# A hybrid encoder layer on one core: an expert's index made apart from its gather, the router written in order by hand, and another issue order for the mixer

## The chip, the cores and the metric

The kernel runs on one core of one Trainium2 chip. The metric is the time of one execution of the whole program on the device, in microseconds. Engines are named as in the profile: PE (matrix multiply; PEld its weight loads), DVE (vector), ACT (activation functions), POOL (the general engine, which also makes the descriptors of gathers and scatters), SP (which issues the plain DMAs).

## The reference

One layer on a sequence of 1024 tokens of width 1024, all in float32 (norms, biases and gains left out here):

```
n = rms_norm(h);  proj = n @ w_in                    # 1024 x 6720
c = silu(centred_dwconv(proj[:, :4608], 7 taps))     # q, k, v, x, B, C
o = gated_delta(q, k, v) both directions             # 8 heads of 128, chunks of 64
y = ssd(x, B, C) both directions                     # 16 heads of 64 in 2 groups
h = h + [norm(o) * silu(gate), norm(y * silu(z))] @ w_out

n2 = rms_norm(h);  aff = softmax(n2 @ w_router)      # 1024 x 16
vals, idx = top_k(aff.T, 128)                        # each expert takes 128 tokens
for e in range(16):
    xs = n2[idx[e]]
    ye = (silu(xs @ w_gate[e]) * (xs @ w_up[e])) @ w_down[e] * vals[e]
    h[idx[e]] += ye
return rms_norm(h)
```

## The kernel before

Products in float32 are made as three passes of a 32-bit matmul form over a high and a low half: ACT makes the high half of a tile (`whi`, or `place` in the experts), DVE subtracts it from the raw tile to get the low half (`wlo`), and PE multiplies high by high, high by low and low by high.

**The mixer.** The program is a list of small jobs, each with a slot, entered with `at(slot, fn, ...)`; a job that yields goes on later. `flush("mixer")` does not follow the slots: it issues the jobs in the order of a table of 3602 numbers, `ORDER["mixer"]`, and `tc.manual_schedule()` around it keeps that order on every engine. The transposed input `n_hi`, `n_lo` is made first (lines 325 to 361): x tiles and the small parameter rows are loaded by SP, PE transposes them, ACT and DVE split them. Then 53 blocks of 128 columns of `w_in` go through `w_load` (SP), `w_split` (ACT `whi`, DVE `wlo`; each block in two halves, 106 in all) and `w_unit` (line 242 on PE, eight times six matmuls for a block). Between them run the convolutions (`cacc`, `cpr`), the delta rule and the scan. The scan's decay tiles `E` are loaded from `rowsD` by SP, masked by POOL in two instructions, put through Exp by ACT and used by DVE; of the 32 tiles, 16 belong to each of two groups. Last come the output projection in six rounds (line 1289), the residual and the router's logits `lg`.

**The router.** After the table's last job the probabilities `aff` are made, and 15 rounds `j` search for each expert's threshold: DVE makes a mask of three trial values (`msk`), PE sums it over tokens (line 1533, eight small matmuls), DVE picks (`best`) and makes the next trial. This part of the code stands outside `manual_schedule`, so there the framework's scheduler orders the instructions. Beside the rounds the first expert's first six weight tiles are split: ACT makes `hi` (`EARLY`), and DVE makes `lo` in 12 halves of 128x512 (`rest`, the function's calls come from the rounds). Then the positions `posx` are worked out.

**The experts.** `flush("moe")` orders its jobs by slot, 17 slots an expert. `rt(e)` makes a one-hot tile `oh` (eight DVE instructions), counts on PE (line 1580), makes the index `idx` and the value on DVE (`ax`), and issues the gather of the expert's 128 rows on POOL (`place<-n2D,idx`). `xt` transposes the rows, `gm` multiplies by gate and up, `ht` transposes, `dm` multiplies by down, `ys` scatters. Weight tiles of 512 KB come through one pool of 46 tiles: `give` returns a tile and issues the next load on SP.

Of the kernel before, what the change touches and what calls it, by code (L numbers as in the profile page):

```python
# [20 lines left out]
L = 1024  # L21
# [22 lines left out]
        "c-l>v1FU9EvxU35tGlY-v2EM7ZQHhO+qP}nwr$(it@HlLmzyVR)#}x?_nyflXELLdQQ=i2<&;)Y6)CH{3a40wQn3_>;;9%yY!zCCQDIdC6-UKY"  # L44
        "5mjUrP^hA-#G*vviB)_RMN%S_OGQ%&RdSU>6ko_Gq*4ilgerH?Q>Z*Duga%Vs?;h;kQORUkn}=Y*-Ed9sB)6hs&ql}tE56vQ8J;Js-rT<%%BR0"
        "G71GnnN@L>No7$BRJI`5h4MmHRY+A(g;fc;%_LiyRY_G!l~!f`qvHSbGOCiQEM7%b6|W|$rD_NJ>Z*pMnyRzpW~!d5FSD$wE0k58R2T98(IDsz"
        "|2vme6I55#O?6j2R8JKO8cEYwHBr4(Q%TK*R;s1ytNN&Zs<mpPdaG%wtu#|qe>FgSq8g|MsljT93JvX4d(}Zrl8qTcXy~Yhso`pbx-O?O5Dvma"
        "1PB9RVW^5I9tk4DR5enKQlr%vHCaW0v1*)}suDpohz@gAbeO4*L0Pz>W~*6hj*1HDAsu9Z7!Xs)2$>)j#D+K!7iO!uDjsBp_>ce+LKe88ZmFy="
        "UR@P(LJ}wk*HjKsE|{n0tIaAKY*q_ZQb-DkVUe1ywy4CA401zq$OF?=dH5|&3P=fgAs^(20+0$)!(z2W{Zu#AFCjZr5Gui6RSEtn1xwX3wOs8~"
        "D^x*PsVYK6NCRo1FsxFQVYOPL0M@E?YO7kWHmHq4P57g#KoxNf$7LReLQn(@REACJkV3cwyOjk8JJfEqN9|Jw)G64j_N$_BP@RS|a28HLF*pf_"  # L50
        ")nRo+*rtxELHZ<|gF0|r9aAUNNp(t{hYN5KPOIWj0!qReRZ6r=U54$dD%60>@EXpk^YUvstFFOyxB=DSg1V%t!7I1|SK$q86|W9&;T^n(4{%Xk"
        "R#((bxCQs%wh97w)E#wK-BWkqBYc8;sut9Sx=;`93wKq0xUcT32I38&5j=tisuPqJzYAZXF*Jck>XCY=9;>F%3?9Q{Nl&0TJW(y+DYS%E@K8Nb"
# [56 lines left out]
def trunk(ctx, tc, x, norm1_w, w_in, conv_w, conv_b, gdn_A_log, gdn_dt_bias, gdn_norm_w,  # L109
# [1376 lines left out]
    act(lg, lg, AF.Exp)  # L1486
    act(warm, mhalf[:, :1], AF.Silu)
    den = hp.tile([128, NT], F32, name="den")
    V.tensor_reduce(den, lg, axis=AX.X, op=OP.add)
# [17 lines left out]
    def rest(parts, cols, last):  # L1507
        raw, hi, lo = parts
        tt(V, lo[:, cols], raw[:, cols], hi.bitcast(F32)[:, cols], OP.subtract)
        if last:  # L1510
            give(raw)
# [322 lines left out]
```

## Time and profile before

| | us |
|---|---|
| median of 3 runs (1672.53, 1676.93, 1685.21) | 1676.93 |
| the profiled execution | 1671.89 |
| its span, first to last instruction | 1670.2 |
| PE busy in the span (93%) | 1550.8 |
| DVE, ACT, POOL busy | 1211.5, 982.0, 730.0 |

A row of the timeline has the start, the time (of all instructions of a merged row, which overlap a little), the engine, line and operation, out<-in with the program's names, and in brackets the idle time of the engine before it and what ended that. PEclk is the granted clock of PE as a share of 2.4 GHz; 0.50 is the lower of its two levels, 1.2 GHz.

### The profile page before, as it was taken

What the parts mean: (1) busy time and instruction counts of PE and PEld (TensorE: products, weight loads), DVE (VectorE), ACT (ScalarE), POOL (GpSimd) and SP (SyncE); (2) the same over time, 40 slices, a digit from 0 to 9 for tenths busy, and PEclk for the clock granted to TensorE, in tenths of its full rate; (3) what the DMA queues carried; (4) which work ended last, traced back from release to release, by engine and by line L of the source; (5) the groups of instructions that cost most, each with busy time, mean ns of one, the idle gap of its engine ahead of it and who ended that gap; (6) DMA issues with size and microseconds to landing.
All of it is one profiled execution on the core that took longest, in us unless ns stands there. A gap on an engine that the chain in (4) does not pass through costs nothing. (4 is left out here: it accounts for less than half of the span.)

```text
span 1670.2 us, 23559 instructions
## 1 busy us (share of the span) xinstructions
PE 1550.8 (93%) x8290; PEld 1264.7 (76%) x8290; DVE 1211.5 (73%) x2045; ACT 982.0 (59%) x1788; POOL 730.0 (44%) x533
## 2 busy tenths in 40 slices
PE   5989999999999999998989999998996499899997
PEld 4768888888889888887765687687885377677774
DVE  4686768686767677757779976864556598789875
ACT  5476485858586767465542574243455177677764
POOL 1285263647454654425898877713032011111112
PEclk9999999999999999999999999999997599999999
DMA  4322223223231322222332245457787289999955
GB/s 137 98 60 43 45 65 68 75 56 87 42 98 28 105 70 63 39 70 95 108 101 70 67 135 172 150 183 263 256 284 291 111 311 372 329 382 375 389 184 213
DMA packets 174784, 254.20 MB, mean 152 GB/s; under 512 B 54370, under 2 KB 112027, under 8 KB 174667
## 3 DMA queue, kind: packets, MB, share of 16 engines
q1 hardware_dynamic: 170202, 236.45, 42.3%
q0 software_dynamic: 4464, 16.25, 3.8%
q8 instruction: 65, 1.06, 0.3%
q14 instruction: 53, 0.43, 0.1%
HBM read 221.01 MB, written 31.65 MB: 151 GB/s over the span
## 5 line engine op out<-in xcount | busy, mean ns | idle before, releaser
L242 PE MATMUL pj<-n,whi 128*128 128x512 f32 x1664 | 482.5, 412 | 9.8 <-ACT whi L129 7.5
L242 PEld LDWEIGHTS pj<-n,whi 128*128 128x128 f32 x1664 | 301.0, 190 | 79.2 <-ACT whi L129 11.1
L242 PE MATMUL pj<-n,wlo 128*128 128x512 f32 x832 | 263.4, 398 | 3.6 <-DVE wlo L123 3.5
L123 DVE TENSOR_TENSOR place<-place 128x1024 fp32r<-128x1024 f32 (+1 forms) x182 | 208.0, 1184 | 27.8 <-ACT place L129 27.8
L126 DVE SCALAR_TENSOR_TENSOR cacc<-pj,cols,cacc 128x1023 f32<-128x1023 f32 (+2 forms) x156 | 199.3, 1278 | 22.8 <-POOL cacc L123 20.1
L123 POOL TENSOR_TENSOR cacc<-cacc,cpr 128x1021 f32<-128x1021 f32 x60 | 145.7, 2429 | 153.4 <-ACT cacc L129 81.0
L1648 PE MATMUL pj<-place 128*128 128x512 f32 x768 | 198.3, 410 | 2.0 <-DVE place L123 1.3
L129 ACT ACTIVATE place<-place 128x1024 fp32r<-128x1024 f32 (+1 forms) x181 | 181.5, 1053 | 16.8 <-issue 8.5
L242 PEld LDWEIGHTS pj<-n,wlo 128*128 128x128 f32 x832 | 156.2, 189 | 45.8 <-DVE wlo L123 8.3
L1648 PEld LDWEIGHTS pj<-place 128*128 128x128 f32 x768 | 144.5, 192 | 40.6 <-DVE place L123 5.3
L123 DVE TENSOR_TENSOR n<-n 128x1024 fp32r<-128x1024 f32 x64 | 84.3, 1327 | 68.9 <-ACT n L129 40.7
L1591 POOL DMA_INDIRECT place<-n2D,idx x16 | 17.4, 1088 | 259.4 <-ACT place L129 93.7
L129 ACT ACTIVATE n<-n 128x1024 fp32r<-128x1024 f32 x64 | 66.7, 1056 | 104.1 <-DMA n<-in_w_out_dram 55.2
L123 DVE TENSOR_TENSOR wlo<-wraw,whi 128x512 fp32r<-128x512 f32 x106 | 96.7, 914 | 15.0 <-ACT whi L129 14.9
L1289 PE MATMUL pj<-n 128*128 128x512 f32 x384 | 97.4, 408 | 4.1 <-DVE n L123 4.1
L129 ACT ACTIVATE whi<-wraw 128x512 fp32r<-128x512 f32 x106 | 65.8, 625 | 57.7 <-PE pj L242 47.5
L129 ACT ACTIVATE place<-g 128x512 fp32r<-128x512 f32 (+1 forms) x48 | 26.9, 561 | 110.4 <-PE g L1612 106.2
L1289 PEld LDWEIGHTS pj<-n 128*128 128x128 f32 x384 | 72.5, 191 | 24.2 <-DVE n L123 5.8
L129 ACT ACTIVATE cpr<-pj,cols 128x1021 f32<-128x1021 f32 x60 | 66.5, 1109 | 26.6 <-PE pj L242 16.9
L129 ACT ACTIVATE u<-c,bt 128x128 f32<-128x128 f32 x128 | 39.6, 363 | 60.1 <-DVE ud L123 58.4
L123 POOL TENSOR_TENSOR ex<-N,nm 128x512 f32<-128x512 f32 x48 | 62.2, 1304 | 14.6 <-PE g L785 9.9
L123 DVE TENSOR_TENSOR E<-E,tb_dt 128x1024 f32<-128x1024 f32 x32 | 56.9, 1790 | 15.5 <-ACT E L129 15.3
(328 smaller groups left out, 3202.9 us busy)
## 6 DMA issues: line engine op xcount, KB each, us to landing
place<-in_w_gate_dram SPq DMA_DIRECT2D x64, 512.0 KB, 9.3
place<-in_w_up_dram SPq DMA_DIRECT2D x64, 512.0 KB, 8.7
place<-in_w_down_dram SPq DMA_DIRECT2D x64, 512.0 KB, 9.8
wraw<-in_w_in_dram SPq DMA_DIRECT2D x106, 256.0 KB, 3.3
E<-rowsD SPq DMA_DIRECT2D x32, 512.0 KB, 3.8
n<-mixD SPq DMA_DIRECT2D x64, 256.0 KB, 3.4
n<-in_w_out_dram SPq DMA_DIRECT2D x64, 256.0 KB, 4.4
dec<-rowsD SPq DMA_DIRECT2D x16, 512.0 KB, 7.7
```

The costliest lines, as they stand in the source:

```text
L123: eng.tensor_tensor(o, a, b, op=op)
L126: V.scalar_tensor_tensor(o, a, s, b, op0=op0, op1=op1, **kw)
L129: S.activation(o, i, f, **kw)
L242: T.matmul(pj[c0][:, hs], lhsT=w[:, d % 4, :], rhs=nn[d][:, hs], start=(d == 0 and a == 0), stop=(d == ND - 1 and a == 2))
L1289: T.matmul(wst["po", r][t], lhsT=m[:, 0, ts], rhs=w[:, 1, :], start=(k == k0 and a == 0), stop=(k == k1 - 1 and a == 2))
L1591: nc.gpsimd.indirect_dma_start(out=ex["xs", e], out_offset=None, in_=n2D[:, :], in_offset=ex["idx", e])
L1648: T.matmul(po, lhsT=xT[:, j, d % 4, :], rhs=wt[k][:, HALF[dd]], start=(d == 0 and a == 0), stop=(d == ND - 1 and a == 2))
```

## The change

Three things change together.

- The table `ORDER["mixer"]` has the same 3602 entries in another order; most jobs stand a little elsewhere.
- The router's code stands inside `tc.manual_schedule()`. The rounds `j` 2 to 13 take one half of `rest` each, the rounds 0 and 1 the two steps of `aux` (the parts of `aff` in a shorter format).
- The gather is a job of its own, `gx(e)`. `rt` of the experts 0 to 3 runs right behind the positions, one after the other with short pauses; `gx` of 0 and 1 stands between them, `gx` of the later experts where the gather stood before.

```
-        "c-l>v1FU9EvxU35tGlY-v2EM7ZQHhO+qP}nwr$(it@HlLmzyVR)#}x?_nyflXELLdQQ=i2<&;)Y6)CH{3a40wQn3_>;;9%yY!zCCQDIdC6-UKY"
+        "c-lRe1CX@65`}|KI+@S5ZQHhO+qP}nwr$(CZCm&3)L*xrI*rqvytBJCyR$-QVTBjrgc3$L5lX}Y@kD45UW65KL?jVGL=`bWY!OjJ7A&L)BLad%"
...
+    with tc.manual_schedule():
         act(lg, lg, AF.Exp)
         act(warm, mhalf[:, :1], AF.Silu)
...
         for j in range(15):
             tt(V, msk3, aff[:, :, None, :].to_broadcast(S4), trialf[:, None].to_broadcast(S4), OP.is_ge)
-        if j > 1 and halves:
-            rest(*halves.popleft())
+            if j < 2:
+                src = res if j else aff
+                V.tensor_copy(aux[:, :, :, 2 + j], src)
+                tt(V, aux[:, :, :, 4] if j else res, src, aux[:, :, :, 2 + j], OP.subtract)
+            elif halves:
+                rest(*halves.popleft())
...
-    res = hp.tile(SE, F32, name="res")
-    V.tensor_copy(aux[:, :, :, 2], aff)
-    tt(V, res, aff, aux[:, :, :, 2], OP.subtract)
-    V.tensor_copy(aux[:, :, :, 3], res)
-    tt(V, aux[:, :, :, 4], res, aux[:, :, :, 3], OP.subtract)
...
     def rt(e):
...
-        yield 6.0
+        yield 0.5 if e < 4 else 6.0
...
-        yield 0.2
+        ex["idx", e], ex["val", e] = bass.IndirectOffsetOnAxis(ap=idx[:, :1], axis=0), ax[:, 6:7]
+
+    def gx(e):
         ex["xs", e] = take()
-        ex["idx", e], ex["val", e] = bass.IndirectOffsetOnAxis(ap=idx[:, :1], axis=0), ax[:, 6:7]
         nc.gpsimd.indirect_dma_start(out=ex["xs", e], out_offset=None, in_=n2D[:, :], in_offset=ex["idx", e])
...
-    at(-30, rt, 0)
-    at(-29, rt, 1)
+    for e in range(4):
+        at(-30 + 1.9 * e, rt, e)
+        if e < 2:
+            at(-28.8 + 1.9 * e, gx, e)
...
             if e + 2 < NE:
-                at(b + 2, rt, e + 2)
+                if e > 1:
+                    at(b + 2, rt, e + 2)
+                at(b + 8.7, gx, e + 2)
```

ACT's queue at the start, behind the splits of the last input tiles (`n`; `whi` are halves of projection weights, `Rf` 128x48 holds the decay parameters that SP loads, `O` is a copy of the first projected block). Before:

```order
L129 ACTIVATE n<-g,cols 128x512 x2
L129 ACTIVATE whi<-wraw 128x512
L129 ACTIVATE n<-g,cols 128x512 x9
L129 ACTIVATE Rf<-Rf 128x48
L129 ACTIVATE whi<-wraw 128x512
L129 ACTIVATE n<-g,cols 128x512 x2
L129 ACTIVATE O<-pj 128x1024
L129 ACTIVATE whi<-wraw 128x512
L129 ACT_TABLE_LOAD
```

Now:

```order
L129 ACTIVATE n<-g,cols 128x512 x9
L129 ACTIVATE whi<-wraw 128x512
L129 ACTIVATE O<-pj 128x1024
L129 ACTIVATE whi<-wraw 128x512
L129 ACT_TABLE_LOAD
L129 ACTIVATE tb_beta<-qd 128x128
L129 ACT_TABLE_LOAD
L129 ACTIVATE Rf<-Rf 128x384
L129 ACTIVATE whi<-wraw 128x512
L129 ACTIVATE Rf<-Rf 128x48
```

`Rf<-Rf 128x48` stood ahead of the last two `n`; it now stands behind all of them and behind three more halves of weights.

ACT's queue where the scan's first two decay tiles `E` come (`cpr`, `cacc` belong to a convolution, `xk` to the scan's input). Before:

```order
L129 ACTIVATE whi<-wraw 128x512 x2
L129 ACTIVATE cpr<-pj,cols 128x1021
L129 ACTIVATE cacc<-pj,cols 128x1024
L129 ACTIVATE xk<-g 128x4x128 x2
L129 ACT_TABLE_LOAD
L129 ACTIVATE E<-E 128x1024
L129 ACTIVATE xk<-g 128x4x128
L129 ACTIVATE E<-E 128x1024
L129 ACTIVATE whi<-wraw 128x512
```

Now:

```order
L129 ACTIVATE whi<-wraw 128x512
L129 ACTIVATE cpr<-pj,cols 128x1021
L129 ACTIVATE cacc<-pj,cols 128x1024
L129 ACTIVATE xk<-g 128x4x128 x3
L129 ACTIVATE whi<-wraw 128x512
L129 ACT_TABLE_LOAD
L129 ACTIVATE E<-E 128x1024 x2
L129 ACTIVATE whi<-wraw 128x512
```

One more half of weights stands ahead of the two `E`: they are followed by the 79th `whi` before, by the 80th now. On SP the loads of these two tiles stand behind the 78th and the 79th load of `wraw` before, both behind the 78th now.

DVE's queue in the router, the rounds 2 to 4 (`place` 128x512 are the halves of `rest`). Before:

```order
L123 TENSOR_TENSOR msk_11577<-aff,trial 128x384
L123 TENSOR_TENSOR place<-place 128x512
L126 SCALAR_TENSOR_TENSOR best_11578<-c,trial 128x48
L123 TENSOR_TENSOR place<-place 128x512
L1537 TENSOR_REDUCE best_11579<-best_11578 128x16
L123 TENSOR_TENSOR place<-place 128x512
L123 TENSOR_TENSOR trial<-best_11579,digit 128x48
L123 TENSOR_TENSOR place<-place 128x512
L123 TENSOR_TENSOR msk_11577<-aff,trial 128x384
```

Now:

```order
L123 TENSOR_TENSOR msk_11579<-aff,trial 128x384
L123 TENSOR_TENSOR place<-place 128x512
L126 SCALAR_TENSOR_TENSOR best_11580<-c,trial 128x48
L1543 TENSOR_REDUCE best_11581<-best_11580 128x16
L123 TENSOR_TENSOR trial<-best_11581,digit 128x48
L123 TENSOR_TENSOR msk_11579<-aff,trial 128x384
L123 TENSOR_TENSOR place<-place 128x512
```

Before, four halves stand in each of three rounds, one between every two steps; now one half stands in each of twelve rounds, between the mask and the pick that waits for PE.

DVE's queue behind the positions, at the start of the experts. Before:

```order
L126 SCALAR_TENSOR_TENSOR posx<-sel,posx 128x128
L1576 TENSOR_SCALAR oh<-slots,posx 128x128 x16
L1583 COPY ax<-c 128x5
L126 SCALAR_TENSOR_TENSOR idx<-ax 128x1
L123 TENSOR_TENSOR ax<-ax 128x1 x2
L1583 COPY ax<-c 128x5
L126 SCALAR_TENSOR_TENSOR idx<-ax 128x1
L123 TENSOR_TENSOR ax<-ax 128x1 x2
L123 TENSOR_TENSOR place<-g,place 128x512 x2
```

Now:

```order
L126 SCALAR_TENSOR_TENSOR posx<-sel,posx 128x128
L1577 TENSOR_SCALAR oh<-slots,posx 128x128 x8
L1584 COPY ax<-c 128x5
L126 SCALAR_TENSOR_TENSOR idx<-ax 128x1
L123 TENSOR_TENSOR ax<-ax 128x1 x2
L1577 TENSOR_SCALAR oh<-slots,posx 128x128 x8
L1584 COPY ax<-c 128x5
L126 SCALAR_TENSOR_TENSOR idx<-ax 128x1
L123 TENSOR_TENSOR ax<-ax 128x1 x2
L1577 TENSOR_SCALAR oh<-slots,posx 128x128 x8
L1584 COPY ax<-c 128x5
```

The first index stands behind one expert's `oh` in place of two, and the indices of the experts 2 and 3 now stand ahead of the first expert's transposed rows (`place<-g,place`) on DVE, and their counts ahead of its transposes on PE.

Two further moves need no rows. On ACT the Exp of `lg` stood right behind a table load and stands right behind the last scaled rows now, with the table load and the `warm` instruction behind it. On DVE the copy `trial<-digit` stood among the splits of the output projection, where the scheduler had put it, and stands in front of the first mask now.

## Rows read from the trace of the kernel before

**Rows 1.** By stretch: length, busy PE, PEld, DVE, ACT, POOL; clock, DMA share, GB/s.
```profile
48.45:1130.00 1081.55, 1048.64 (x5844) 872.16 (x5843) 809.86 (x1379) 646.65 (x1354) 628.32 (x382) 0.99 0.30 85
1276.40:1325.40 49.00, 11.50 (x146) 8.27 (x145) 32.89 (x115) 8.07 (x9) 2.18 (x2) 0.50 0.58 225
1400.00:1600.00 200.00, 194.17 (x917) 150.57 (x917) 173.37 (x274) 142.85 (x173) 29.12 (x20) 0.98 1.01 372
```

**Rows 2.** Waits of PE from 48.5 to 1276 us: sum, times, longest.
```profile
PE pj L242 <- ACT whi L129: 7.5, 2, 4.6
```

**Rows 3.** Timeline of ACT, then of PE, at the start.
```profile
41.05 0.24 ACT L129 ACTIVATE Rf<-Rf 128x48 f32<-128x48 f32 x1 [6.53 <-DMA Rf<-in_ssd_A_log_dram]
...
42.44 0.50 PE L250 MATMUL pj<-n,whi 128*128 128x512 f32 x1 [3.56 <-ACT n L129]
...
48.45 2.05 PE L242 MATMUL pj<-n,whi 128*128 128x512 f32 x4
...
50.84 1.10 PE L242 MATMUL pj<-n,whi 128*128 128x512 f32 x4
```

**Rows 4.** Timeline of ACT, then of PE, where the scan begins and near its middle.
```profile
784.18 0.61 ACT L129 ACTIVATE whi<-wraw 128x512 fp32r<-128x512 f32 x1
...
784.85 2.07 PE L242 MATMUL pj<-n,whi 128*128 128x512 f32 x4 [2.89 <-ACT whi L129]
786.72 1.05 PE L242 MATMUL pj<-n,wlo 128*128 128x512 f32 x2
...
876.82 2.08 PE L242 MATMUL pj<-n,whi 128*128 128x512 f32 x4 [4.60 <-ACT whi L129]
```

**Rows 5.** Timeline of DVE, then of PE, in the output projection.
```profile
1137.50 0.20 DVE L1526 COPY trial<-digit 128x48 int32<-128x48 int32 x1 [3.52 <-POOL digit L1473]
...
1138.95 12.79 PE L1289 MATMUL pj<-n 128*128 128x512 f32 x48 [2.70 <-DVE n L123]
```

**Rows 6.** Timeline of ACT, then of DVE, at the router's start.
```profile
1277.22 1.28 ACT L129 ACT_TABLE_LOAD   x1
1278.51 0.31 ACT L129 ACTIVATE lg<-lg 128x128 f32<-128x128 f32 x1
...
1277.01 0.23 DVE L123 TENSOR_TENSOR lg<-lg,r 128x64 f32<-128x64 f32 x1
```

**Rows 7.** Timeline of PE, then of DVE, in the router's rounds.
```profile
1280.35 0.48 PE L1533 MATMUL c<-msk,ones_b 128*128 128x48 bf16 x8 [4.32 <-DVE msk L123]
...
1310.20 0.50 PE L1533 MATMUL c<-msk,ones_b 128*128 128x48 bf16 x8 [1.43 <-DVE msk L123]
1312.14 0.50 PE L1533 MATMUL c<-msk,ones_b 128*128 128x48 bf16 x8 [1.43 <-DVE msk L123]
...
1284.52 0.68 DVE L123 TENSOR_TENSOR place<-place 128x512 fp32r<-128x512 f32 x1
1285.20 0.21 DVE L126 SCALAR_TENSOR_TENSOR best<-c,trial 128x48 f32<-128x48 f32 x1
...
1297.21 0.21 DVE L126 SCALAR_TENSOR_TENSOR best<-c,trial 128x48 f32<-128x48 f32 x1 [0.60 <-PE c L1533]
```

**Rows 8.** Timeline of DVE, POOL and PE where the experts begin.
```profile
1316.98 2.69 DVE L1576 TENSOR_SCALAR oh<-slots,posx 128x128 bf16<-128x128 bf16 x16
1319.60 0.15 DVE L1583 COPY ax<-c 128x5 f32<-128x5 f32 x1
...
1320.83 1.25 POOL L1591 DMA_INDIRECT place<-n2D,idx  x1 [45.66 <-DVE ax L123]
1322.38 0.94 POOL L1591 DMA_INDIRECT place<-n2D,idx  x1 [0.30 <-issue]
1338.43 1.43 POOL L1591 DMA_INDIRECT place<-n2D,idx  x1 [15.12 <-PE pj L1648]
...
1325.39 1.98 PE L1612 MATMUL g<-ident,place 128*128 128x128 f32 x8 [5.46 <-DMA place<-n2D,idx]
```

**Rows 9.** SP's queue behind the router: the loads of the gate weights.
```profile
1292.79 44.23 SPq L1443 DMA_DIRECT2D place<-in_w_gate_dram  x4
```

More of the change, by code (lines that the diff above doesn't have):

```diff
@@ L48 @@
[L48 to L52, printed above, removed]
@@ L105 @@
+        ">--+S-yifxphNz=pMvT*+@t=K--Nr?qdS3mvp?f6`8AmAfOo-%4V?97kuUqx{+yrcH~5XHulgH)o4@TZ`bqv8c;c`4>;5LV<?s2O{-M7E?)v-S"
+        "k$(U^^^bkHz*GOsKld+if5<&seN{gP-An)4hYxJ<lYM1B+kf$|(7*DZ{2Tukdgp)m_lOY!-~3FRdgr$XPe%+y3PcV>34HZY10S&Y%YVe)2jssX"
+        "<irO!(E=a+XaC3l#FO3!9T5<L+5Wfx?*D=4ff#|9fmngqfjEJ<fj>T8;D6dIGVc",
 }
@@ L1485, in trunk @@
     aff, ones_b, before_b, slots, aux, posx, lg = (tv[n] for n in ("aff", "ones_b", "before_b", "slots", "aux", "posx", "lg"))
[L1486 to L1489, printed above, removed]
-    V.reciprocal(den, den)
-    tt(V, aff, lg, den[:, :, None].to_broadcast(SE), OP.mult)
-    mp = pool("mp")
-    ex = {}
-    halves = deque()
-    def split(w, e, i):
-        raw = eraw.pop(epos[w, e, i])
-        if (w, i) in WHOLE:
-            ex["w", w, e, i] = raw,
-            return None
-        hi, lo = take(F32R), take(F32R)
-        ex["w", w, e, i] = hi, lo
-        act(hi, raw, AF.Copy)
-        return raw, hi, lo
@@ L1507, in rest @@
[L1507 to L1511, printed above, removed]
-    EARLY = [(w, 0, i) for w in range(2) for i in range(3)]
-    for key in EARLY:
-        parts = split(*key)
-        halves.extend((parts, HALF[h], h) for h in range(2))
-    msk3 = hp.tile([128, NT, 3, NE], BF, name="msk3")
-    best = [hp.tile([128, 4, NE], F32, name=f"best{i}") for i in range(2)]
-    trial = hp.tile([128, 3, NE], I32, name="trial")
@@ L1521, in trunk @@
-    S3 = [128, 3, NE]
-    S4 = [128, NT, 3, NE]
-    trialf = trial.bitcast(F32)
-    over3 = lambda a: a[:, :, None].to_broadcast(S3)
-    V.memset(best[0][:, 0, :], 0.0)
-    V.tensor_copy(trial, over3(tv["digit"][:, 0, :]))
-    for j in range(15):
-        tt(V, msk3, aff[:, :, None, :].to_broadcast(S4), trialf[:, None].to_broadcast(S4), OP.is_ge)
-        if j > 1 and halves:
-            rest(*halves.popleft())
-        pc = ctile([128, 3, NE])
-        for t in range(NT):
-            T.matmul(pc.rearrange("p k e -> p (k e)"), lhsT=ones_b, rhs=msk3[:, t].rearrange("p k e -> p (k e)"),
-                     start=(t == 0), stop=(t == NT - 1))
-        stt(best[j % 2][:, 1:4, :], pc, 127.5, trialf, OP.is_ge, OP.mult)
-        thr = best[1 - j % 2][:, 0, :]
-        V.tensor_reduce(thr, best[j % 2].rearrange("p k e -> p e k"), axis=AX.X, op=OP.max)
-        if j < 14:
-            tt(V, trial, thr.bitcast(I32)[:, None, :].to_broadcast(S3), over3(tv["digit"][:, j + 1, :]), OP.bitwise_xor)
@@ L1541, in trunk @@
-    ge = hp.tile([128, NT + 1, 2, NE], BF, name="ge")
-    gt, eq = ge[:, 1:, 0, :], ge[:, 1:, 1, :]
-    P.memset(ge[:, 0], 0.0)
-    thr_b = thr[:, None, :].to_broadcast(SE)
-    tt(V, gt, aff, thr_b, OP.is_gt)
-    tt(V, eq, aff, thr_b, OP.is_equal)
-    gf = ge.rearrange("p t k e -> p t (k e)")
-    pb = gtile([128, NT + 1, 2 * NE])
-    T.matmul(pb, lhsT=ones_b, rhs=gf, start=True, stop=False)
-    T.matmul(pb[:, :NT], lhsT=before_b, rhs=gf[:, 1:], start=False, stop=False)
-    for u in range(1, NT):
-        T.matmul(pb[:, u + 1:], lhsT=ones_b, rhs=gf[:, 1:NT + 1 - u], start=False, stop=(u == NT - 1))
```

198 lines of the change are left out of this document (130 added, 68 removed).

## The prediction

> **What bounds the kernel now.** I read the table of stretches first, because the change touches three stages with different limits. In the mixer, 48.45 to 1130 us, PE is busy 1048.64 of 1081.55 us at a clock of 0.99 [rows 1]: PE is the bound there, and all that another order can win directly is the 32.9 us in which it is idle. In the router, 1276.4 to 1325.4, PE is busy 11.50 of 49 us and DVE 32.89 [rows 1]. No engine is full; the limit is a chain from DVE's mask to PE's sum and back to DVE's pick, and each instruction taken out of that chain counts in full. In the experts, 1400 to 1600, PE is busy 194.17 of 200 us, and the DMA engines are full at 1.01 [rows 1]. Then I read PE's waits. Only two waits for weights in the whole mixer, 7.5 us together, the longest 4.6 [rows 2], are large and have a single cause. The third view is the timeline around each of them, at the start, in the router and where the experts begin.
>
> **The change part by part.** The sum is made against the profiled execution, 1671.89 us.
>
> *The start.* ACT waits 6.53 us for a small load ahead of `Rf` 128x48; two `n` stand behind it in ACT's queue, and PE waits 3.56 us for the first of them [rows 3]. Then PE is slow: the same four matmuls take 2.05 us at 48.45 and 1.10 at 50.84 [rows 3]; the granted clock is at its lower level, 1.2 GHz, after the pause. `Rf` now stands behind all the `n`, so the wait goes. If no other pause follows, the slow stretch of 42.44 to 50.84 goes too; of these 8.4 us at most a share of 1 − 1.10/2.05 = 0.46, thus 3.9 us, is lost to the clock. I take half of it, because the copy `O` still stands between the first block and its use and may leave a pause of its own: −3.56 − 1.95 = −5.5 us, with bounds of 0 (a later load becomes the wait in place of this one) and −7.5. What is late next is `Rf` itself, and behind it only `whi` for blocks that come later.
>
> *The mixer's other jobs.* At 784.85 PE waits 2.89 us for a `whi` that ACT makes at 784.18, behind the first two `E` [rows 4]. After it, four matmuls take 2.07 in place of 1.10, and two 1.05 in place of 0.55 (half of four): 0.97 + 0.50 = 1.5 us lost to the clock. In the new order one more half of weights stands ahead of the two `E` on ACT, which is 24 matmuls for PE, at 1.10 us for four some 6.6 us of cover, more than 2.89; and SP issues the second `E` load earlier. I take this stall as gone: −2.89 − 1.5 = −4.4 us. The other stall, 4.60 us at 876.82 [rows 4], I leave as it is, since there, too, `whi` stands behind an `E` on ACT in the new order. Nearly all the other entries of the table have moved as well, and the trace of before can't price them one by one. I take zero for their sum, since PE is already at 97% here and a stall removed elsewhere can be one put in; the bounds are half of the idle 32.9 us, −16, and two new stalls of the kind at 876.82, each 4.60 and, as twice the 1.5 above, 3 in slow matmuls, 7.6 together, +15.
>
> *The output projection.* The scheduler had put `trial<-digit` among the splits; it waits 3.52 us for POOL there, and soon after PE waits 2.70 us for an `n` that DVE splits behind it [rows 5]. Now the copy stands in the router. The wait of PE is shared with others, since DVE has been idle ahead of that split for other reasons too: 0 to −2.7, I take half, −1.3 us.
>
> *The router's table load.* `lg` is ready at 1277.01 + 0.23 = 1277.24, and ACT begins a table load at 1277.22 that ends where Exp begins, at 1278.51 [rows 6]. The load is there because the scheduler had put `warm` (Silu) ahead of Exp. Now Exp comes first and the load lies behind it, where ACT has no one waiting: −1.2 us (1278.51 − 1277.24, less a little).
>
> The Trainium skill ("ScalarE: Activation LUTs", What ACT_TABLE_LOAD costs) states about 1.28 us for the load and 1.38 more for a drain, 2.66 for a switch. The row agrees with the first part and contradicts the second here: Exp begins 1.29 us after the load. By the page this term would be −2.7, by the row it is −1.2.
>
> *The rounds.* From the first sum at 1280.35 to the last at 1312.14 are 31.79 us for 14 periods; a period without a half takes 1312.14 − 1310.20 = 1.94 us [rows 7]. Without halves in the chain it would be 14 × 1.94 = 27.2, so 4.6 us are lost to the three rounds that hold four halves each. A half takes 0.68 [rows 7]. Between mask and pick DVE waits 0.60 us for PE [rows 7], and in a round with a half there, the pick at 1285.20 starts as the half ends [rows 7]; a single half there thus costs at most 0.08, in twelve rounds 1.0 us. Halves placed elsewhere would be in the chain in full; now none is. On the other side stand three short instructions that come into the chain (the memset, the copy, and what of `aux` reaches past the wait), each put at about 0.2 like the copy's row [rows 5]: +0.5. The result is −4.1 us, with bounds of −3.1 (all halves reach out) and −4.6. The cover of a half is the wait for PE: if PE were quicker there, 0.68 each would come back.
>
> *Index and gather.* `oh` for two experts takes 2.69 us ahead of the first `ax` [rows 8]; now the first index waits for eight `oh`, 1.35, so the first gather comes about 1.3 us sooner. But the counts of the experts 2 and 3 now stand ahead of the first transposes on PE, and they wait for their `oh`. On DVE an expert takes 1.35 for `oh`, 0.6 for index and value (two of them lie between the first `ax` at 1319.60 and the gather at 1320.83 [rows 8]) and up to 0.3 of waiting for the count, an estimate; four take 7.8 to 9.0 behind 1316.98, so the last count is done at about 1324.2 to 1325.4 and DVE at 1324.8 to 1326.0. The transposes start at 1325.39 now, waiting for the gather [rows 8]. So the wait for the gather is replaced by one for DVE that ends at nearly the same time: −0.2, bounds −0.9 and +1.4. Later the experts 0 and 1 lose 1.4 us of `oh` on a DVE that doesn't bound there: nothing.
>
> *The loads.* SP's group of gate loads at 1292.79 lasts 44.23 us [rows 9], because the tiles that it fills come free only as the first expert runs on PE. So what the router gives, the loads get too, and the experts begin earlier as a whole.
>
> Sum: −5.5 − 4.4 − 1.3 − 1.2 − 4.1 − 0.2 = −16.7, thus 1655.2 against 1671.89. The four executions shown (the profiled one, 1672.53, 1676.93, 1685.21) have their middle at 1674.7, 2.8 above the profiled one: **1658 us**.
>
> **Rivals.**
>
> *The order brings nothing net.* The start and the stall at 784.85 are answered by new waits of the same size: only −1.3 − 1.2 − 4.1 − 0.2 = −6.8 is left, 1667.9. For it: one late load stops PE at the start, and the loads aren't faster.
>
> *The order brings more.* A third of the idle 32.9 us goes beside the terms above, the stall at 876.82 with it: 11 to 13 less, about 1646.
>
> *Slower: the scan's masks.* A `whi` that stands on ACT behind an `E` waits for POOL's mask, as at 876.82, where PE lost 4.60 us and about 3 at the low clock [rows 4]. If the new order puts `E` of the scan closer together on ACT, so that there are four or more such stalls than now, at 7.6 us each 30 us, the time is about 1689. It decides as soon as three more stalls (23 us) outweigh the 16.7. Against it: PE shows only two waits for `whi` in the trace of before [rows 2], and the table has the same jobs.
>
> *The gathers held up.* A gather's instruction takes 0.94 us while DVE is idle at 1322.38, and 1.43 at 1338.43, while DVE splits weights [rows 8]. Now both first gathers are issued while DVE makes `oh`: 0.5 more for each and the transposes wait for it again, +1.0 to 1.5, so 1659.5.
>
> The Trainium skill ("SBUF — State Buffer", SBUF: two separate sides) states that VectorE and GpSimd share a port pair as an exclusive lock, so that descriptors of a DMA issued by GpSimd wait for VectorE in its two-port modes. The 1.43 against 0.94 fits it; whether `oh` counts as such an instruction no run here shows.
>
> *The experts give it back.* Where DMA is the bound of the experts (1.01 [rows 1]), an earlier start on PE's side would be lost to the loads: 6.8 us less of gain, 1665. Against it: the loads stop for PE, not PE for the loads, in the 44.23 us [rows 9].
>
> **How the numbers follow.** The forecast has a chance of 0.47, the order without net effect 0.20, more from the order 0.14, the masks 0.08, held-up gathers 0.05, the experts 0.06. The range of 1643 to 1677 takes in all but the masks (0.08) and the further half of "more" (0.07), and the bounds of the unknown moves as far as +15 and −16 reach. One per cent, 16.8 us, is about what a measurement of this kernel can tell from no change. Faster by more than that is below 1660.2: 0.30 of the forecast's 0.47 and 0.14, thus 0.44; within it 0.17 + 0.20 + 0.05 + 0.06 = 0.48; slower 0.08.
>
> **What would show it.** Start: no wait of 3.56 at PE's last blocks of the first unit, four matmuls at 1.10 before 48 us. Scan: no wait of PE for `whi` at the first `E`; if one stands there, that step fails. Router: Exp of `lg` directly behind the last scaled `n`; 14 periods in 27 to 28.5 us, each with one half. Experts: the first transposes wait for a count or DVE, not for a gather, about 8 us behind the first `oh`. The prediction is wrong if PE's idle time in the mixer differs from 32.9 − 10 by more than about 10 us, if the slow-clock stretches remain or multiply there, or if the experts take longer than before between first transposes and the end.

## The result, and the profile after

The changed kernel takes 1655.77 us (four executions, 1654.9 to 1656.91) against 1677.95 for the kernel before (four, 1672.53 to 1685.21): a ratio of 0.9865, with a 95% interval of 0.9827 to 0.9904. Forecast were 1658 and a range of 1643 to 1677. In a later comparison (e9) the same kernel gave 0.9895 (0.987 to 0.992), 1662.95 against 1678.83; both readings are used below.

The profiled execution has a span of 1653.2, 17.0 less than before. Landmarks on PE divide it; each is the start of an instruction, but for the end of the output projection. The stretches between them, worked out from the timelines of three profiled executions:

| stretch on PE, us | before | after | after, e9 |
|---|---|---|---|
| start to the first unit of weights (line 242) | 48.45 | 42.90 | 44.17 |
| to the end of the output projection | 1218.42 | 1215.47 | 1223.22 |
| to the first sum of the rounds | 13.48 | 11.74 | 11.74 |
| rounds: first to last sum | 31.79 | 27.09 | 27.10 |
| to the first transposes of an expert | 13.25 | 13.19 | 13.19 |
| to the end | 344.81 | 342.81 | 342.68 |

Five of the six rows repeat within 1.3 us in the two executions of the changed kernel. The second, which holds nearly all of the reordered jobs, differs by 7.8 us between them. That is the main thing to read out of this case. The third row repeats here, but not everywhere: with the same router it is 11.95 in e6, 12.25 in e5 and 14.37 in e2, and in e2 the matmuls ahead of the last logits ran slow. What repeats is its part from the last logits (the last eight matmuls that make `lg`) to the first sum.

The stretches of the profile after, with the columns of [rows 1]; the last two rows are from a cut at this kernel's own landmarks:

```profile
48.45:1130.00 1081.55, 1048.83 (x5862) 876.05 (x5861) 811.89 (x1380) 642.91 (x1352) 633.28 (x416) 0.99 0.30 87
1400.00:1600.00 200.00, 194.22 (x909) 150.59 (x907) 171.78 (x262) 143.76 (x175) 28.12 (x19) 0.98 0.96 348
...
1270.10:1297.20 27.10, 6.98 (x113) 5.17 (x112) 25.52 (x72) 5.55 (x6) 0.00 (x0) 0.50 0.91 362
1310.40:1653.20 342.80, 321.21 (x1465) 245.94 (x1465) 275.03 (x409) 228.90 (x285) 51.23 (x38) 0.98 0.87 314
```

The mixer's row is the one to compare with [rows 1]: busy 1048.83 where it was 1048.64 of the same 1081.55. The prediction's sign of being wrong was an idle time of PE more than about 10 us away from 32.9 − 10; it is 32.7, which is 9.8 away. The same columns for the second row of the table, before, after and in e9:

```profile
48.45:1266.87 1218.42, 1180.86 (x6483) 981.95 (x6481) 877.54 (x1454) 710.47 (x1441) 663.17 (x464) 0.99 0.35 104
...
42.90:1258.37 1215.47, 1177.27 (x6483) 982.29 (x6481) 876.01 (x1451) 706.30 (x1438) 660.66 (x466) 0.99 0.34 103
...
44.17:1267.39 1223.22, 1183.72 (x6483) 986.89 (x6481) 880.05 (x1451) 706.51 (x1438) 660.63 (x466) 0.99 0.34 103
```

PE's idle time in it is 37.6, 38.2 and 39.5 us. It did not fall; the 2.95 us that the stretch is shorter in the first profile are busy time, and e9 has more of that than the kernel before. PE's waits say where the idle time went (columns as in [rows 2]; PE from 0 to 1260 us):

```profile
PE c L1168 <- DVE hs L123: 6.0, 2, 5.2
...
PE c L1118 <- DVE E L123: 2.4, 1, 2.4
PE g L1058 <- POOL E L123: 1.8, 1, 1.8
...
PE pj L242 <- ACT whi L129: 0.2, 1, 0.2
```

The 7.5 us for `whi` of [rows 2] are 0.2 now, and three waits of the scan have come: for `hs`, 5.2, and for `E`, twice. The start, on ACT and then on PE, which answers [rows 3]:

```profile
35.39 1.27 ACT L129 ACTIVATE n<-g,cols 128x512 fp32r<-128x512 f32 x2 [1.16 <-PE g L359]
...
38.68 0.51 PE L250 MATMUL pj<-n,whi 128*128 128x512 f32 x1 [1.26 <-DVE n L126]
41.28 1.97 PE L471 MATMUL g<-ident,O 128*128 128x128 f32 x8 [1.16 <-ACT O L129]
42.90 1.81 PE L242 MATMUL pj<-n,whi 128*128 128x512 f32 x4
...
45.02 1.09 PE L242 MATMUL pj<-n,whi 128*128 128x512 f32 x4
```

The wait of 3.56 has become 1.26; the pause for `O`, 1.16, stays, and the first four matmuls behind it are still slow (1.81 against 1.09). The router's start on ACT, then the rounds on PE and DVE, which answer [rows 6, 7]:

```profile
1265.05 3.21 ACT L129 ACTIVATE n<-n,r 128x1024 f32<-128x1024 f32 x3
1268.17 0.29 ACT L129 ACTIVATE lg<-lg 128x128 f32<-128x128 f32 x1
1268.48 1.28 ACT L129 ACT_TABLE_LOAD   x1
...
1295.26 0.50 PE L1539 MATMUL c<-msk,ones_b 128*128 128x48 bf16 x8 [1.43 <-DVE msk L123]
1297.20 0.50 PE L1539 MATMUL c<-msk,ones_b 128*128 128x48 bf16 x8 [1.43 <-DVE msk L123]
...
1267.25 0.22 DVE L123 TENSOR_TENSOR lg<-lg,r 128x64 f32<-128x64 f32 x1
...
1273.86 0.68 DVE L123 TENSOR_TENSOR place<-place 128x512 fp32r<-128x512 f32 x1
1274.53 0.21 DVE L126 SCALAR_TENSOR_TENSOR best<-c,trial 128x48 f32<-128x48 f32 x1
```

A round with a half in it takes 1.94, like one without. `lg` is ready at 1267.47, and Exp starts at 1268.17, because three scaled rows stand ahead of it on ACT. The start of the experts on POOL and PE, which answers [rows 8]:

```profile
1304.97 1.25 POOL L1593 DMA_INDIRECT place<-n2D,idx  x1 [38.45 <-DVE oh L1577]
1307.10 0.95 POOL L1593 DMA_INDIRECT place<-n2D,idx  x1 [0.89 <-DVE oh L1577]
...
1309.21 1.32 PE L1581 MATMUL c<-aux,oh 128*128 128x5 bf16 x8 [0.88 <-DVE oh L1577]
1310.39 1.95 PE L1614 MATMUL g<-ident,place 128*128 128x128 f32 x8
1312.22 6.66 PE L1650 MATMUL pj<-place 128*128 128x512 f32 x24
```

The transposes no longer wait for the gather; what precedes them is the fourth expert's count, which waits for its `oh`.

### The profile page after: what moved, and what is told of

Read it like the earlier page. It is cut to its first block, busy times and chain, and to the rows that moved or that the text cites. A ratio compares the mean times of both kernels' runs of the same rounds, so it can differ in the third digit from the quotient of the medians.

```text
span 1653.2 us, 23559 instructions
## 1 busy us (share of the span) xinstructions
PE 1545.5 (93%) x8290; PEld 1264.7 (77%) x8290; DVE 1212.1 (73%) x2045; ACT 976.1 (59%) x1784; POOL 727.2 (44%) x533
## 5 line engine op out<-in xcount | busy, mean ns | idle before, releaser
L129 ACT ACTIVATE place<-place 128x1024 fp32r<-128x1024 f32 (+1 forms) x181 | 181.4, 1053 | 15.9 <-issue 8.3
L1593 POOL DMA_INDIRECT place<-n2D,idx x16 | 16.7, 1044 | 247.2 <-ACT place L129 108.5
L123 DVE TENSOR_TENSOR wlo<-wraw,whi 128x512 fp32r<-128x512 f32 x106 | 100.4, 950 | 26.2 <-ACT whi L129 22.4
L123 POOL TENSOR_TENSOR E<-E,tb_gc 128x1024 f32<-128x1024 f32 x32 | 67.8, 2119 | 6.8 <-DMA E<-rowsD 6.8
```

Source lines behind the costliest of these rows:

```text
L123: eng.tensor_tensor(o, a, b, op=op)
L129: S.activation(o, i, f, **kw)
L1593: nc.gpsimd.indirect_dma_start(out=ex["xs", e], out_offset=None, in_=n2D[:, :], in_offset=ex["idx", e])
```

## The experiments

All comparisons are with the kernel before on the same chip. Its median was 1677.66 (27 executions) for e1 to e4, 1680.36 (7) for e5 to e8 and 1678.83 (21) for e9 to e12.

### The order and the code apart: e1, e2

e1 is the kernel before with the new table, e2 the changed kernel with the old one.

```
 e1, in the kernel before:
-ORDER["mixer"] of before
+ORDER["mixer"] of after
 e2, in the changed kernel:
-ORDER["mixer"] of after
+ORDER["mixer"] of before
```

> The kernel before with the new table alone; router, index and gather as before. Theory (each wait that goes is worth its own length on PE): about 8.5 us shorter than before up to the last matmul of the output projection (5.8 at the start, 2.7 behind it), the rounds at 31.8, the experts from the first transposes to the end at 344.8: about 1661.5 for the span. Rival (the experts, whose DMA share is 1.01, give the earlier start back): the stretch behind the first transposes grows by 4 us or more, about 1666.

> The changed kernel with the old table. Theory: rounds 27.1, experts from the first transposes to the end 342.8, the wait of PE at the start (3.56) and the two waits for weights in the scan (2.89, 4.60) back: 8 us less than before, a span of about 1662. Rival (the router's gain needs the new order ahead of it, since the loads and the splits of the first expert come no earlier): the halves of the first expert wait, less than 4 us gained, 1667 or more.

e1: 1670.51, ratio 0.9958 (0.9935 to 0.9981). e2: 1666.55, ratio 0.9924 (0.9897 to 0.9951). The two multiply to 0.9882, which lies between the two readings of the whole change: nothing here says that one part needs the other, and neither rival holds. By the medians the code is worth more than the order; the intervals overlap. In e1 the rounds take 31.78 and the experts 344.76; in e2 they take 27.09 and 342.57. The start is 43.31 and 49.29. e1 was forecast at 8.5 and gave 7.1 us; e2 at 8, and gave 11.1. Part of the latter is the copy `trial<-digit` that no longer stands in the output projection. In e2, with the old table, PE's wait there and the matmuls behind it are:

```profile
1144.45 11.18 PE L1289 MATMUL pj<-n 128*128 128x512 f32 x48 [1.38 <-DVE n L123]
```

[Rows 5] had 2.70 and 12.79 for the same 48: 1.3 us of waiting and 1.6 of slow matmuls. The forecast had the first alone. Rounds 4.7, experts 2.2, copy 2.9, the way from the last logits to the first sum 1.1 (6.20 to 5.08) and the positions 0.3 add up to 11.2, each read from one profile, against the 11.1 by the medians.

### The order in two pieces: e3, e4

e3 has the new order up to the first load of a decay tile, e4 the new order from there on; what is left follows in the old order.

```
 e3: +jobs of the new table ahead of e_load (0, 0)
     +the jobs left, as in the old table
 e4:  jobs of the old table ahead of e_load (0, 0)
     +the jobs left, as in the new table
```

> The kernel before with the new table up to the first load of a decay tile and the old order of what is left behind it. Theory: the 5.8 us of the start stay, because PE is the bound up to there, and both waits for weights come back unchanged: about 5.5 less than before, a span of 1664.7. Rival (the scan is bound by POOL's masks, which start at their own time): the waits for weights grow by what PE gained, less than 2 us left.

> The kernel before with the old table up to the first load of a decay tile and the new order behind it. Theory: the wait at the start stays, both waits of PE for weights in the scan go (7.5 and 4 to 5 at the low clock), others of 5.2 and 2.4 come as in the changed kernel: 2.7 to 4 less than before, a span of about 1667. Rival (the new scan needs the earlier part of its own table): waits for weights remain, 0 or slower.

e3: 1670.16, ratio 0.9959 (0.9933 to 0.9986), as much as the whole new order; the waits for `whi` are back, 7.9 us in three, but have not grown by what the start gave, so the rival falls. e4: 1676.34, ratio 0.9982 (0.9966 to 0.9998), 1.3 us by the medians. What the order brings, by the medians, is won ahead of the scan. The scan's own new order is worth 0 to 6 us by the interval, which holds the 2.7 to 4 expected of e4 and is barely clear of zero. In e4's profile the waits for `whi` are down from 7.5 to 1.3 us, and PE's idle time from the first unit to the end of the output projection is 40.0 us, not less than before.

### One job at the start: e11

```
 x_turn (1, 6) step 1 ... b0
 rates step 1
-rates step 2          # Exp of Rf 128x48
-rates step 3
 ...
 scal1 step 12
+rates step 2
+rates step 3
```

> The kernel before with one edit of the table: the Exp of the decay parameters (Rf 128x48) and the step behind it stand behind all the splits of the inputs, as in the new order. Theory (the start is won by this one move): the first unit's first matmuls at 42.5 to 43.5 in place of 48.45, a gain of 5.5 us against before, about 1672. Rival (other moves of the start count as much): the first unit at 46 or later.

1672.83, ratio 0.9978 (0.9957 to 1.0). The first unit starts at 44.37, 4.1 earlier than in [rows 3]; the wait that is left is one for DVE:

```profile
40.92 0.51 PE L250 MATMUL pj<-n,whi 128*128 128x512 f32 x1 [0.92 <-DVE n L126]
...
44.37 1.18 PE L242 MATMUL pj<-n,whi 128*128 128x512 f32 x4
```

That lies between the theory's 42.5 to 43.5 and the rival's 46. By the medians the move gives 6.0 us, and its interval reaches up to no gain. The nine profiles with the new order at the start have the first unit at 42.13 to 44.17, four with the old one at 48.45 to 49.58. So this one job is most of the start's gain, and whether the other moves there add to it can't be told, since one start differs by 2 us between executions.

### The waits for weights in the scan: e12

Two splits of weights are moved ahead on ACT, in the kernel before. The first has the wait of 2.89 of [rows 4], the second that of 4.60.

```
+w_split (5632, 0) step 1
 e_exp (0, 0)
 ...
 e_exp (1, 1)
-w_split (5632, 0) step 1
 ...
+w_load (4480, 1)
+w_split (4480, 1) step 1
 e_exp (6, 0)
 ...
 e_exp (7, 0)
-w_load (4480, 1)
-w_split (4480, 1) step 1
```

> The kernel before with two splits of weights moved ahead on ACT, the one of the wait of 2.89 ahead of the first two E, the one of the wait of 4.60 ahead of the two E it stood behind. Theory of the prediction (each such wait is worth its length and the slow matmuls behind it): both waits of PE for whi gone, 9 to 12 us shorter in the scan, about 1667. Rival (POOL's chain of masks sets the pace of the scan, and PE's idle time only changes its place, as in the changed kernel, where a wait of 5.2 for hs stands in for them): other waits of PE come in the scan, less than 4 us gained.

1679.13, ratio 1.0009 (0.9989 to 1.0028): nothing. The waits of PE from 48.5 to 1276 show what came instead; in the kernel before the same two lines have 3.5 and 2.1 us:

```profile
PE pj L242 <- DVE wlo L123: 9.2, 5, 6.1
PE pj L242 <- DVE cacc L126: 5.0, 5, 2.9
```

Both waits for `whi` are gone, and two of the same length or longer stand in their places: 2.86 for `cacc` at 787.67 and 6.07 for `wlo` at 882.69. On ACT, then on DVE, ahead of the first:

```profile
781.89 0.63 ACT L129 ACTIVATE whi<-wraw 128x512 fp32r<-128x512 f32 x1 [6.75 <-DMA wraw<-in_w_in_dram]
...
783.83 1.06 ACT L129 ACTIVATE E<-E 128x1024 f32<-128x1024 f32 x1
...
784.92 1.41 DVE L123 TENSOR_TENSOR E<-E,tb_dt 128x1024 f32<-128x1024 f32 x1 [2.94 <-ACT E L129]
```

Here the moved half waits 6.75 us for its own load, and the `E`, which stand behind it on ACT, come later for that; DVE's `cacc` stands behind the `E`. The second `E` load starts 2.85 us later than in the kernel before (775.14 against 772.29), and PE's wait ends 2.82 later: at the same point of the program. So at the first place the edit made a delay of its own, and e12 doesn't show what the wait is worth where the load comes in time. On DVE, then on ACT, around the second:

```profile
879.75 2.29 DVE L123 TENSOR_TENSOR E<-E,tb_dt 128x1024 f32<-128x1024 f32 x1 [2.07 <-ACT E L129]
881.96 0.68 DVE L123 TENSOR_TENSOR wlo<-wraw,whi 128x512 fp32r<-128x512 f32 x1
...
878.66 2.00 ACT L129 ACTIVATE E<-E 128x1024 f32<-128x1024 f32 x2 [2.68 <-POOL E L560]
```

The low half of the same weights stands on DVE behind three `E`, DVE waits for ACT's `E`, and ACT waits 2.68 for POOL's mask. Taking ACT out of this chain leaves DVE in it. In the scan, from 770 to 1040 us, POOL is busy 227.3 of 270 us in the kernel before, and 227.2 of 270, from 765 to 1035, in the changed one. That its masks set the pace there is likely by this; no run makes them quicker.

### Index and gather: e5

The changed kernel, with index and gather of the first experts as before.

```
-        yield 0.5 if e < 4 else 6.0
+        yield 6.0
...
-    for e in range(4):
-        at(-30 + 1.9 * e, rt, e)
-        if e < 2:
-            at(-28.8 + 1.9 * e, gx, e)
+    for e in range(2):
+        at(-30 + e, rt, e)
+        at(-23 + e, gx, e)
...
-                if e > 1:
-                    at(b + 2, rt, e + 2)
+                at(b + 2, rt, e + 2)
```

> The changed kernel, but index and gather as before: experts 0 and 1 have their indices made together, both gathers behind them, and the counts of experts 2 and 3 come inside the experts 0 and 1. Theory (two counts of 0.35 us on a full PE, a wait of 0.5 for DVE, and the first product of 24 matmuls at the low clock, 0.6): from the first transposes to the end 344.8 as before, up to the first transposes unchanged, a span 2.0 longer than the changed kernel's 1653.2. Rival (the 2.0 come from the splits being done earlier, by the rounds): 342.8 stays.

1661.48, ratio 0.9897 (0.9859 to 0.9936). From the position stage to the first transposes nothing changes (13.09). From there to the end it takes 346.99, longer than the theory's 344.8. That stretch differs between executions, but the two kinds of code keep apart: 344.8 to 347.9 in the six profiles with the old index and gather beside e5 (before, e1, e3, e4, e11, e12), 342.6 to 344.1 in the seven others (after, e2, e6 to e10). The rival, 342.8, falls. The stretch up to the transposes behind the longest stall repeats better: they start 102.36 us after the first ones, in the kernel before 102.56, and 100.06 in the changed kernel. The places of these 2.3 us: two counts of 0.35, which stand no longer among the matmuls of a full PE; one wait for DVE, 1.31 before and 1.30 in e5, which is 0.81; one wait for ACT's `place`, 0.35 before and 0.45 in e5, which is gone, with 0.4 of slower matmuls behind it; and the first product of 24 matmuls, 6.66 in the changed kernel, 6.97 in e5 and 7.30 before. The last is the clock and not the change: over the fourteen profiles this product takes 6.4 to 7.8 with either code.

### The rounds: e6

Four halves again in each of three rounds, in the hand-written order.

```
             stt(best[j % 2][:, 1:4, :], pc, 127.5, trialf, OP.is_ge, OP.mult)
+            if 1 < j < 5:
+                rest(*halves.popleft())
...
             V.tensor_reduce(thr, best[j % 2].rearrange("p k e -> p e k"), axis=AX.X, op=OP.max)
+            if 1 < j < 5:
+                rest(*halves.popleft())
             if j < 14:
                 tt(V, trial, ...)
+                if 1 < j < 5:
+                    rest(*halves.popleft())
```

> The changed kernel with four halves in each of the rounds 2, 3 and 4, one behind each step, and none in the others. Theory: three periods of 3.36 in place of 1.93, so 14 periods take 31.4 in place of 27.1, and the span is 4.3 longer, 1657.5. Rival (what shortened the rounds is the hand-written order of the other instructions): 27 to 28 stays.

1661.6, ratio 0.9904 (0.987 to 0.9938). The rounds take 31.37. A packed period and a plain one, on PE:

```profile
1275.92 0.50 PE L1539 MATMUL c<-msk,ones_b 128*128 128x48 bf16 x8 [1.50 <-DVE msk L123]
1279.28 0.50 PE L1539 MATMUL c<-msk,ones_b 128*128 128x48 bf16 x8 [2.86 <-DVE msk L123]
...
1301.46 0.50 PE L1539 MATMUL c<-msk,ones_b 128*128 128x48 bf16 x8 [1.43 <-DVE msk L123]
1303.40 0.50 PE L1539 MATMUL c<-msk,ones_b 128*128 128x48 bf16 x8 [1.43 <-DVE msk L123]
```

3.36 against 1.94: the place of the halves gives 4.3 of the 4.7 us of the rounds.

### The table load and the Exp: e7, e8

e7 makes the earlier `warm` a Silu and drops the later one. e8 puts Exp ahead of the last scaled rows, and the halves one round later; in e8 one tile's rows are also scaled and stored ahead of half of their multiplication by the second norm's weights, which is thus left out of its result.

```
 e7:
-            act(warm, mhalf[:, :1], AF.Exp)
+            act(warm, mhalf[:, :1], AF.Silu)
...
         act(lg, lg, AF.Exp)
-        act(warm, mhalf[:, :1], AF.Silu)
```

```
 e8, with flush("mixer") and the router in one manual_schedule:
 r_lg (1)
+r_n2 (5), (7), (6), (4), both steps, taken from places ahead and behind
...
         tt(V, lg, lg, b4(tv["r2"][:, t4]), OP.mult)
+        if th == 1:
+            act(tv["lg"], tv["lg"], AF.Exp)
...
-        act(lg, lg, AF.Exp)
...
-            elif halves:
+            elif j > 2 and halves:
```

> The changed kernel, but the earlier warm instruction is Silu and the later one is left out, so that the table load stands ahead of the Exp of the logits, as before. Theory: Exp starts 1.29 us behind the last scaled rows in place of directly behind, so the first sum comes 1.3 later and the span is 1.3 longer, 1654.5; the last scaled rows hold Exp by 0.7 in the changed kernel, so against a free ACT the load would cost only 0.6. Rival (by the Trainium skill, ScalarE: Activation LUTs, What ACT_TABLE_LOAD costs, a switch is 2.66): 2.7 longer.

> The changed kernel with the Exp of the logits ahead of the last four scalings of rows on ACT, and the halves in the rounds 3 to 14. Theory: Exp no longer waits 0.7 for the scalings, and PE's 0.7 wait for ACT ahead of the last logits goes: the first sum comes 1.2 earlier, a span of 1652.0. Rival (the splits of the first expert come 4 us later on ACT and the halves wait for them): the rounds grow, no gain or a loss of 1 to 3.

e7: 1662.64, ratio 0.9899 (0.9857 to 0.994). ACT, then PE:

```profile
1268.78 3.21 ACT L129 ACTIVATE n<-n,r 128x1024 f32<-128x1024 f32 x3
1272.01 1.28 ACT L129 ACT_TABLE_LOAD   x1
1273.30 0.31 ACT L129 ACTIVATE lg<-lg 128x128 f32<-128x128 f32 x1
...
1268.94 1.89 PE L1335 MATMUL pj<-wr,n 128*128 128x16 f32 x8 [0.69 <-ACT n L129]
1275.26 0.48 PE L1538 MATMUL c<-msk,ones_b 128*128 128x48 bf16 x8 [4.44 <-DVE msk L123]
```

The same on PE in e5, which has the router of the changed kernel:

```profile
1268.33 1.89 PE L1335 MATMUL pj<-wr,n 128*128 128x16 f32 x8 [0.69 <-ACT n L129]
1273.42 0.48 PE L1539 MATMUL c<-msk,ones_b 128*128 128x48 bf16 x8 [3.20 <-DVE msk L123]
```

Exp starts 1.29 behind the load's start and no drain is seen, so the 2.66 of the rival (the Trainium skill, "ScalarE: Activation LUTs", What ACT_TABLE_LOAD costs) isn't met here. From the last logits to the first sum are 6.32 us in e7. With the same slow logits, 1.89, the router without the load ahead of Exp takes 5.09 in e5 and 5.08 in e2 and e6; in the two profiles of the changed kernel the logits are quick, 1.07, and it takes 4.91. So the load costs 1.2 to 1.4 on the path, as the first half of the theory says. The second half, 0.6, doesn't hold. The scaled rows hold Exp by 0.7 only where the logits are quick; where they are slow, `lg` is ready 3.09 behind their start and the rows end 3.05 behind it. And the load stands behind the rows, so with it Exp is late by the whole load in either case.

e8: 1660.11, ratio 0.9888 (0.9855 to 0.9921). Its logits are slow, 1.89, and from them to the first sum are 5.09, as in e5: at these logits Exp gains nothing by standing ahead of the rows. PE's 0.69 wait for ACT stays, since it is that of the last logits for their own copy, and the rounds take 27.52, 0.43 more. So nothing is won, as the rival has it, but not for its reason alone. The times of e5 to e8 lie within 2.6 us of one another, and their intervals overlap; what is said of them rests on stretches of one profile each.

### One kernel's executions, and PE kept busy: e9, e10

e9 is the changed kernel again. e10 adds matmuls whose result nobody reads; there, too, the mixer's jobs and the router stand in one `manual_schedule`, so that the added matmuls stay where they are written.

```
+        pspare = psum.tile([128, L], F32, name="pj", tag="pj")
+        def busy(n):
+            for i in range(n):
+                T.matmul(pspare[:, HALF[i % 2]].rearrange("p (a c) -> p a c", c=128), lhsT=ones_b,
+                         rhs=before_b[:, None, :].to_broadcast(C4), start=True, stop=True)
+        busy(8)
         for j in range(15):
...
+            busy(3)
             stt(best[j % 2][:, 1:4, :], pc, 127.5, trialf, OP.is_ge, OP.mult)
...
+        busy(6)
```

> The changed kernel once more, beside the next three on one chip, to see how one program's executions differ. Theory (the executions differ by how long PE is granted 1.2 GHz, about 1.4 us for 0.001 of mean clock as in the executions of before): a median of 1656 to 1660, and within the kernel a longer time goes with a lower mean clock. Rival (they differ by the chip alone): all within 2 us, whatever the clock.

> The changed kernel with matmuls of 512 columns that nobody reads added to PE in the router: 8 ahead of the first sum, 3 behind each round's sum, 6 behind the positions. Theory (PE's clock is low there because it waits between short sums): granted clock in the rounds above 0.5, the sum of 0.50 us at 0.3 to 0.4, a period of 1.8 in place of 1.93, and the first product of 24 matmuls 5.8 in place of 6.7: 2 to 4 us shorter than the changed kernel. Rival (the added matmuls stand in front of the sums, at 0.43 each at 1.2 GHz, or the clock doesn't follow them): period 1.93 or longer, no gain or a loss of up to 3.

e9: 1662.95 (five executions, 1656.25 to 1664.54), mean granted clock 0.971 to 0.976; in the first comparison the same program had 1654.9 to 1656.91 at 0.974 to 0.978. The rival that all lie within 2 us on one chip falls; the theory's median of 1656 to 1660 is missed too, and over these five the link to the clock is loose (1658.64 at 0.971, 1662.95 at 0.974). It is seen best where there are many executions: 27 of the kernel before, 1671.86 to 1686.28 at 0.971 down to 0.963, fall 1.4 us for each 0.001 of clock, with a correlation of −0.88. Work on a full PE would lose 1.7 us for it: 0.001 of 1676 us is 3.35 us at 1.2 GHz, and half of that is lost. In the two profiles of the changed kernel PE is idle 107.7 (1653.2 − 1545.50) and 109.7 us (1662.1 − 1552.45), but busy 7.0 longer in e9, with the same instructions. In the kernel before it is idle 119.4. So the idle time tells the programs apart, 10 to 12 us, and the busy time mostly tells how long PE was granted the lower clock.

e10: 1658.97 (1654.54 to 1663.83), ratio 0.9883 (0.986 to 0.9906), mean clock 0.979 to 0.986. A sum and the added matmuls, late in the rounds:

```profile
1302.21 0.37 PE L1546 MATMUL c<-msk,ones_b 128*128 128x48 bf16 x8 [0.83 <-DVE msk L123]
1302.42 0.81 PE L1532 MATMUL pj<-before_b,ones_b 128*128 128x512 bf16 x3
1304.06 0.37 PE L1546 MATMUL c<-msk,ones_b 128*128 128x48 bf16 x8 [0.82 <-DVE msk L123]
```

The granted clock in the rounds is 0.93 in place of 0.50, a sum takes 0.37 in place of 0.50, a period 1.85 in place of 1.94. The rounds take 26.14 and the stretch to the first transposes 12.46: 1.7 us less than in e9. The first product of 24 matmuls, forecast at 5.8, takes 7.30, and the stretch ahead of the first sum 14.28, 2.5 more than in e9; the matmuls there ran slow already ahead of the added ones. By the time it is 4 us faster than e9 on the same chip, but with five executions of each the intervals overlap; that it beats the changed kernel is likely, and not shown.

## Why the prediction was right, and where not

The total, 1658 against 1655.77 and 1662.95, came out of six terms. Four held to about a microsecond, one was mis-sized, one failed, and a gain of the experts was missing.

- **The start.** Forecast −5.5, measured −5.6 in the first profile (48.45 to 42.90), −4.3 in e9. The cause is the one given (e11). Part of the loss to the clock stayed in these two, behind the pause for `O`, as the term allowed. But the pause alone doesn't decide it: in e6, e8 and e10 the same pauses, 1.26 and 1.16, are followed by four matmuls in 1.18 or 1.19, and e8, which reaches `O` at the same 41.28, is 1.4 us ahead by the second four.
- **The stall at 784.85, −4.4.** This step failed. It said that one more half of weights ahead of the `E` pair would cover the wait, and it did; the wait for `whi` went, at 876.82 too. But it took a wait that goes for time that is won. PE's idle time from the first unit to the end of the output projection is 37.6 before, 38.2 and 39.5 after: other waits came. In the changed kernel 5.2 for `hs` and 4.2 for `E` stand in the scan; ahead of the `hs`, DVE's queue has `E`, and ACT waits 2.92 for POOL's mask of one of them. e12 removes both waits alone and gains nothing: at the second place `wlo` waits behind such `E`, at the first the moved half waits for its load. That the new scan order is worth a little is not excluded (e4, 0 to 6 us). The rest of the order, taken as zero, wasn't seen apart from zero either: the stretch is 2.95 shorter in one profile and 4.8 longer in the other.
- **The hoisted copy, −1.3.** Mis-sized: with the old table it is 1.3 of waiting and 1.6 of slow matmuls, 2.9 (e2). The term left out the clock, which the start's term had counted. In the new order the output projection has other waits (1.17, 1.15, 1.15), and its gain isn't seen there.
- **The table load, −1.2.** Held: 1.2 to 1.4 by e7 against e5, e6 and the changed kernel. From the last logits to the first sum are 6.20 to 6.21 in all six profiles with the old router, slow logits or quick, 5.08 or 5.09 with the new one and slow logits, 4.91 with quick ones. What the term overlooked is that the last scaled rows stand ahead of Exp on ACT and hold it by 0.7 where the logits are quick. The rest of the 1.74 by which the stretch fell, 0.45, lies ahead of the last logits.
- **The rounds, −4.1.** Measured −4.7, just outside the bound of −4.6; e6 shows that the place of the halves does 4.3 of it. The bound of 1.0 us for halves reaching out of the wait didn't come to bear (1.94 in both kinds of round).
- **Index and gather, −0.2.** Measured −0.06. Behind it stood the sentence that experts 0 and 1 lose their `oh` and that this is worth nothing; that was wrong by 2.3 us (e5). It looked at DVE alone. The counts also leave PE, which is full there, and go to a stretch in which PE waits.
- **The order brings nothing net**, a rival, is right on the stall and wrong on the start.
- **Held-up gathers** were a rival. The two gathers beside `oh` take 1.25 and 0.95, those of [rows 8] with DVE idle 1.25 and 0.94, so `oh` doesn't hold them up. The rule behind it, that VectorE in its two-port modes holds up such a gather's descriptors (the Trainium skill, "SBUF — State Buffer", SBUF: two separate sides), is not met at `oh`.
- **The experts give it back** and **the masks make it slower**: neither happened. The experts became shorter, and of the waits for `whi` 0.2 us are left.

That the total came so near is partly luck. Against the profile of before, the first profile of the changed kernel has 2.95 where 5.7 was forecast for the stretch with the reordered jobs, and 2.0 in the experts where nothing was: together 17.0 for the forecast 16.7. In e9 that stretch is 4.8 longer than before, and the whole is 8.1 shorter. And the allowance of 2.8 for a fast profiled execution was too small: the kernel before has its median at 1678, 6 above that execution. By the medians the change gave 22.2 us in the first comparison and 15.9 in e9.

## What to carry to other kernels

A wait that stands on the full engine is worth its length only if no other engine's queue, behind the same slower chain, makes it wait at nearly the same time; before counting it, follow the queue of the next engine that needs that chain, and afterwards look at the idle time of the whole stretch and not at the wait that went. When a step moves, count what it frees on every engine, the full one first, and not only on the engine that it is named after. Where executions of one program differ by more than the terms that are argued, compare the stretches of several profiles and split PE's time into idle and busy, because here the idle time showed the program and the busy time mostly the clock.

## What the runs showed of the hardware

The granted clock differs from execution to execution of one program on one chip: 0.963 to 0.971 over 27 executions of the kernel before; at 1.4 us for 0.001 that is about 11 of its range of 14 us. A fall of the clock isn't fixed by the program: behind the same two pauses at the start, 1.26 or 1.27 and 1.16 us, the first four matmuls of the first unit take 1.81 to 2.06 in six of nine profiles and 1.18 or 1.19 in three. PE's clock in the rounds can be raised by work that nobody reads: with it, 14 of the 15 sums ran at 0.37 or 0.36 us, and without it they take 0.50 at a granted clock of 0.50. A table load of 1.28 us ahead of Exp was followed by it at once in the kernel before and in e7. A gather of 128 rows takes 0.94 us with DVE idle, the first one 1.25. Where it begins while DVE subtracts two tiles of 128x1024, it takes 1.43 and 2.03 (before, at 1338.43 and 1375.98) and 1.75 (after, at 1335.28); one that begins 0.05 us ahead of such a subtraction takes 0.99 (before, at 1395.15).
